# Odd layer of a 1024-token model: grouped heads before the latent ones, each set of heads prepared under other work

## The chip, the cores and the metric

One core of a Trainium2 chip runs the whole program in one launch. The metric is device microseconds of that core; less is better. Engines: TensorE (PE), VectorE (DVE), ScalarE (ACT), GpSimd (POOL); SyncE (SP) issues most of the transfers.

## The reference, cut to what matters

A first block (three mixers and a dense MLP) is followed by a second one of two layers, an even and an odd one, each a mixer and a mixture of 16 experts. The change is in the mixer of the odd layer, over 1024 tokens of width 1024:

```
def mixer_odd(h, pos, row, col, w_in, cq_norm, w_cq_up, ckv_norm, w_ckv_up, dq_norm, dk_norm, w_out):
    proj = h @ w_in                                   # 1184 columns
    cq, ckv, ck_rope, dq, dk, dv = jnp.split(proj, [o1, o2, o3, o4, o5], axis=-1)
    cq = (rmsnorm(cq, cq_norm) @ w_cq_up).reshape(b, s, C_HEADS, C_NOPE + C_ROPE)
    q_nope, q_rope = cq[..., :C_NOPE], rope(cq[..., C_NOPE:], pos, ROPE_THETA)
    kv = (rmsnorm(ckv, ckv_norm) @ w_ckv_up).reshape(b, s, C_HEADS, C_NOPE + C_V)
    k_nope, v_c = kv[..., :C_NOPE], kv[..., C_NOPE:]
    k_rope = rope(ck_rope, pos, ROPE_THETA)
    ...
    c_out = block_attention(q_c, k_c, v_c)
    dq = axial_rope(rmsnorm(dq.reshape(b, s, D_KV_HEADS, D_GROUP, HEAD_DIM), dq_norm), row, col)
    dk = axial_rope(rmsnorm(dk.reshape(b, s, D_KV_HEADS, HEAD_DIM), dk_norm), row, col)
    ...
    d_out = block_attention(dq, dk, dv)
    return jnp.concatenate([c_out, d_out], axis=-1) @ w_out
```

There are 8 latent heads (c: queries of 64 + 32 columns made from 256 low-rank columns, keys and values from 128) and 8 grouped heads (d: 64 columns, two heads of keys and values, four query heads to each). Softmax is over all 1024 keys.

## The kernel before

All matrices are float32; a product is made of three matmuls over operands split into a rounded high part and the rest (`mm3`, lines 91 to 93; `split_into`, lines 98 and 99: ACT copies the high part, DVE or POOL subtracts). Tokens lie on the partitions, in 8 tiles of 128.

Order of the odd layer in `program`: `norm_T` norms and transposes the rows into `h`; `odd_proj` makes the 1184 columns in five groups, the 416 latent ones into `cc` and then the 768 grouped ones into `dd`, and stops once between for `odd_c_in`, which norms the latent columns under the rest of the projections. `odd_c` transposes the low-rank columns (line 1744), and traces `odd_d_in` (norm and rotation of the grouped queries and keys, tile by tile, lines 1698 to 1702 and 1072 to 1077) at low priority. Then for each of two groups of four latent heads it makes the queries of all of them (line 1799), rotates them on POOL, and makes the values; each of these projections goes through the one PSUM bank `pj` and is read out of it by ACT and DVE. Head by head it stacks keys and queries (`stacks`) and runs the attention of the head before. Then the rows of the output weights are loaded and split (`w_rows`), and `odd_d` stacks the keys (line 369) and queries (line 361) of the grouped heads, a pair of heads at a time, and runs their attention. `out_moe` multiplies with the output weights, tile by tile; the 128 rows of the attention's output that come last (`late`) are loaded apart and used last.

`attn_head` takes a head in four units of two query tiles (256 rows). For each tile: scores into a pair of banks, the minimum (the queries are negated) on DVE (line 1038), exponential and sum on ACT (line 1041), transposition of the 1024 weights by PE (line 396) and their split (the second half by ACT and POOL, lines 400 to 402, into `pt`, of which there are three buffers). Then 16 matmuls with the values (lines 1048 and 1049), and the scaling, which POOL ends (line 1058) before the result goes to DRAM (`cD`, line 1060).

The order of the instructions on each engine is set before the run by a planner: it takes the order of the program text as priority and fills in, by estimated durations, what is ready by its own clock. On the chip each engine then works its list in that order.

Of the kernel before, what the change touches and what calls it, by code (L numbers as in the profile page):

```python
# [18 lines left out]
NT = 8  # L19
# [7 lines left out]
class Kern:  # L27
# [990 lines left out]
    def attn_head(self, sp, scores, V, dst, row, exp_scale, tab=None):  # L1018
# [3 lines left out]
        for qr in range(4):  # L1022
            pt = self.pt_tiles(sp, 3 if tab is None else 2)
            rc = sp.tile([128, 2], F32, name="arc", tag="arc", bufs=2)
            for qi in range(2):
# [5 lines left out]
                e = sp.tile([128, 1024], F32, name="e", tag="e", bufs=2 if tab is None else 3)  # L1031
                if tab is not None:
                    nc.vector.tensor_tensor_reduce(
                        out=e, in0=pv, in1=tab[:, 896 - 128 * t:1920 - 128 * t],
                        scale=1.0, scalar=3.0e38, op0=ALU.add, op1=ALU.min, accum_out=st[:, 0:1])
                    pv = e
                else:
                    nc.vector.tensor_reduce(out=st[:, 0:1], in_=pv, axis=AX.X, op=ALU.min)  # L1038
                    if exp_scale != 1.0:
                        nc.vector.tensor_scalar(st[:, 0:1], st[:, 0:1], exp_scale, None, op0=ALU.mult)  # L1040
# [648 lines left out]
    def rms_N(self, sp, x, n, g, sq=None):  # L1689

        nc = self.nc
        a = x.shape[1]
        if sq is None:
            sq = sp.tile([128, a * n], F32, name="rsq", tag="qn")
        sq = sq.rearrange("p (a n) -> p a n", a=a)
        ss = sp.tile([128, a], F32, name="rnss", tag="rnss%d" % a)
        rs = sp.tile([128, a], F32, name="rnrs", tag="rnrs%d" % a)
        nc.gpsimd.tensor_tensor(sq, x, x, op=ALU.mult)
        nc.vector.tensor_reduce(out=ss, in_=sq, axis=AX.X, op=ALU.add)
        self.rstd(ss, n, rs)  # L1700
        nc.vector.tensor_tensor(x, x, rs[:, :, None].to_broadcast([128, a, n]), op=ALU.mult)
# [12 lines left out]
    def rope_tab(self, sp, name, half, nh, free=None):  # L1714
        nc = self.nc
        r = []
        for i in range(2):
            if free is None:
# [470 lines left out]
```

## Time and profile before

| | |
|---|---|
| time, median of 3 runs | 4341.29 us (4339.98 to 4341.6) |
| the profiled execution | 4346.24 us, span 4344.5 us |
| PE busy | 3861.5 us, 89% |
| DVE, ACT, POOL busy | 2440.4, 1915.9, 1149.2 us |
| mean granted clock of PE | 0.939 of 2.4 GHz |

Busy time is what an engine spends in instructions; matmuls are pipelined, so a PE that is busy all the time can still be held up a little at each instruction. The span is from the first to the last instruction; the time of the execution is 1.7 us longer.

### The profile page before, as it was taken

What the parts mean: (1) busy time and instruction counts of PE and PEld (TensorE: products, weight loads), DVE (VectorE), ACT (ScalarE), POOL (GpSimd) and SP (SyncE); (2) the same over time, 40 slices, a digit from 0 to 9 for tenths busy, and PEclk for the clock granted to TensorE, in tenths of its full rate; (3) what the DMA queues carried; (4) which work ended last, traced back from release to release, by engine and by line L of the source; (5) the groups of instructions that cost most, each with busy time, mean ns of one, the idle gap of its engine ahead of it and who ended that gap; (6) DMA issues with size and microseconds to landing.
All of it is one profiled execution on the core that took longest, in us unless ns stands there. A gap on an engine that the chain in (4) does not pass through costs nothing. (4 is left out here: it accounts for less than half of the span.)

```text
span 4344.5 us, 57369 instructions
## 1 busy us (share of the span) xinstructions
PE 3861.5 (89%) x21765; PEld 3209.0 (74%) x21765; DVE 2440.4 (56%) x4070; ACT 1915.9 (44%) x3190; POOL 1149.2 (26%) x878
## 2 busy tenths in 40 slices
PE   6999978898799999998999988699895898996997
PEld 5887866666587888886899977576694787884765
DVE  6545584663344233336446673787538566736876
ACT  3444434241424211112455662366523667832765
POOL 2000041330343112124412221011024556620111
PEclk8999989989899999999899998799997999997999
DMA  4212253121543111112242333799410001036997
GB/s 167 72 51 56 85 177 102 49 99 54 203 146 97 54 44 54 44 49 80 61 120 74 85 88 128 280 377 361 150 45 9 18 8 58 19 103 248 375 356 245
DMA packets 321975, 531.40 MB, mean 122 GB/s; under 512 B 39894, under 2 KB 217441, under 8 KB 321700
## 3 DMA queue, kind: packets, MB, share of 16 engines
q1 hardware_dynamic: 312052, 492.62, 33.5%
q0 software_dynamic: 9648, 35.13, 3.2%
q8 instruction: 171, 2.80, 0.3%
q14 instruction: 104, 0.85, 0.1%
HBM read 427.39 MB, written 91.88 MB: 120 GB/s over the span
## 5 line engine op out<-in xcount | busy, mean ns | idle before, releaser
L98 ACT ACTIVATE whi<-wraw 128x1024 fp32r<-128x1024 f32 (+1 forms) x515 | 530.1, 1038 | 777.7 <-PE py L93 213.7
L99 DVE TENSOR_TENSOR wlo<-wraw,whi 128x1024 fp32r<-128x1024 f32 (+3 forms) x418 | 519.0, 1258 | 409.6 <-ACT whi L98 397.2
L99 POOL TENSOR_TENSOR wlo<-wraw,whi 128x1024 fp32r<-128x1024 f32 (+3 forms) x97 | 226.6, 2336 | 1198.0 <-ACT whi L98 1135.7
L91 PE MATMUL pj<-h,whi 128*128 128x512 f32 (+1 forms) x592 | 255.6, 432 | 44.0 <-ACT gst L791 41.8
L92 PE MATMUL mm<-h,whi 128*128 128x512 f32 x640 | 253.9, 397 | 3.0 <-POOL h L99 1.8
L91 PE MATMUL mm<-h,whi 128*128 128x512 f32 x640 | 252.7, 397 | 1.8 <-ACT ms L905 1.4
L93 PE MATMUL mm<-h,wlo 128*128 128x512 f32 x640 | 252.9, 396 | 0.8 <-POOL wlo L99 0.8
L92 PE MATMUL pj<-h,whi 128*128 128x512 f32 (+1 forms) x592 | 248.1, 419 | 0.0
L93 PE MATMUL pj<-h,wlo 128*128 128x512 f32 (+1 forms) x592 | 246.5, 416 | 0.2 <-POOL wlo L99 0.2
L91 PE MATMUL pgu<-whi,xe 128*128 128x512 f32 x512 | 207.6, 406 | 6.2 <-ACT xe L98 6.2
L927 DVE TENSOR_TENSOR Y<-py,Y 128x1024 f32<-128x1024 f32 x112 | 137.1, 1224 | 133.3 <-PE py L93 133.3
L91 PE MATMUL py<-whi,mr 128*128 128x512 f32 x512 | 201.6, 394 | 9.3 <-DVE mr L936 8.2
L93 PE MATMUL pgu<-whi,xe 128*128 128x512 f32 x512 | 205.7, 402 | 0.0
L92 PE MATMUL pgu<-wlo,xe 128*128 128x512 f32 x512 | 205.5, 401 | 0.0
L93 PE MATMUL py<-whi,mr 128*128 128x512 f32 x512 | 203.1, 397 | 0.0
L92 PE MATMUL py<-wlo,mr 128*128 128x512 f32 x512 | 202.4, 395 | 0.0
L396 PE MATMUL ptp<-ident,e 128*128 128x128 f32 x1280 | 183.8, 278 | 15.1 <-ACT pf L400 6.9
L1038 DVE TENSOR_REDUCE ast<-ps 128x1 f32<-128x1024 f32 x128 | 156.4, 1222 | 69.7 <-PE ps L93 48.6
L91 PEld LDWEIGHTS pj<-h,whi 128*128 128x128 f32 (+1 forms) x592 | 118.4, 200 | 85.4 <-ACT gst L791 50.7
L396 PEld LDWEIGHTS ptp<-ident,e 128*128 128x128 f32 x1280 | 149.9, 143 | 30.8 <-ACT pf L400 13.6
L402 POOL TENSOR_TENSOR pt<-pf,pt 128x512 fp32r<-128x512 f32 x128 | 164.0, 1281 | 10.4
L99 DVE TENSOR_TENSOR pt<-ptp,pt 128x512 fp32r<-128x512 f32 x192 | 130.5, 689 | 40.2 <-ACT pt L98 38.9
(643 smaller groups left out, 11038.2 us busy)
## 6 DMA issues: line engine op xcount, KB each, us to landing
wraw<-in_moe_w_gate_dram SPq DMA_DIRECT2D x128, 512.0 KB
wraw<-in_moe_w_up_dram SPq DMA_DIRECT2D x128, 512.0 KB
wraw<-in_moe_w_down_dram SPq DMA_DIRECT2D x128, 512.0 KB
wraw<-in_mlp_w_dram SPq DMA_DIRECT2D x64, 512.0 KB
wraw<-in_w_in_dram SPq DMA_DIRECT2D x52, 512.0 KB
wad<-in_ada_w_dram SPq DMA_DIRECT2D x48, 512.0 KB
gD<-gst SPq DMA_DIRECT2D x24, 512.0 KB
wraw<-x SPq DMA_DIRECT2D x20, 512.0 KB
```

The lines of the kernel that those rows point to most:

```text
L91: t.matmul(out, l[0], r[0], start=start, stop=False)
L92: t.matmul(out, l[0], r[1], start=False, stop=False)
L93: return t.matmul(out, l[1], r[0], start=False, stop=stop)
L98: nc.scalar.activation(hi, src, AF.Copy)
L99: (nc.gpsimd if leng == "pool" else nc.vector).tensor_tensor(lo, src, hi.bitcast(F32), op=ALU.subtract)
L396: nc.tensor.transpose(p[:, k, :], e[:, (4 * kg + k) * 128:(4 * kg + k + 1) * 128], self.ident)
L402: nc.gpsimd.tensor_tensor(lo, f, hi.bitcast(F32), op=ALU.subtract)
L927: nc.vector.tensor_tensor(y, pv, y, op=ALU.add)
L1038: nc.vector.tensor_reduce(out=st[:, 0:1], in_=pv, axis=AX.X, op=ALU.min)
```

## The change

The columns of the projection are reordered: keys and values of the grouped heads first, then their queries, and the latent columns last. The grouped keys and queries are normed and rotated under the following column groups, four tiles and up to four heads to an instruction instead of one tile and ten heads, and the keys are stacked there too. The grouped heads run first, the latent ones after them. `attn_head` calls a function at the beginning of each of its units; `program` and `odd_c` hold tables of what is made at which unit: the norms of the latent columns in units 1 to 3 of the grouped heads, their transposes in 5 to 7, the first group's queries, rotation and values in 9 to 15, the shared key part in 17, and the first latent head's stacks in 25 and 26. In the latent heads, each head's stacks come some units ahead, the second group's queries in units 9 to 11 and its values in 12 and 13. The rows of the output weights are loaded one at a time in seven latent units, and the eighth after the attention. Tiles are in other places of the memory; the last rows of the attention's output are now the fourth 128 (`late` is 3, was 7). The even layer calls the new `w_rows` for the same eight rows.

```
-    def attn_head(self, sp, scores, V, dst, row, exp_scale, tab=None):
+    def attn_head(self, sp, scores, V, dst, row, exp_scale, step, unit):
...
+            step(unit + qr)
+            pt = self.pt_tiles(sp, 3)
...
+        a, b = x.shape[1:3]
+        g = g[:, None, None, :].to_broadcast([128, a, b, n])
...
+            sq = sp.tile([128, 1024], F32, name="rsq", tag="rsq")
+        sq = sq[:, :a * b * n].rearrange("p (a b n) -> p a b n", a=a, b=b)
+        ss = sp.tile([128, a * b], F32, name="rnss", tag="rnss%d" % (a * b))
+        rs = sp.tile([128, a * b], F32, name="rnrs", tag="rnrs%d" % (a * b))
...
+        nc.vector.tensor_reduce(out=ss.rearrange("p (a b) -> p a b", a=a), in_=sq, axis=AX.X, op=ALU.add)
...
+        rs = rs.rearrange("p (a b) -> p a b", a=a)[:, :, :, None].to_broadcast([128, a, b, n])
+        nc.vector.tensor_tensor(x, x, rs, op=ALU.mult)
...
-        for i, (c0, lo) in enumerate(((0, 0), (160, 256), (416, 416), (672, 672), (928, 928))):
-            if i == 2:
-                yield
+        for i, (c0, lo) in enumerate(((928, 928), (416, 416), (672, 672), (0, 0), (160, 256))):
...
+            if lo >= 416:
+                yield
...
-    def odd_c_in(self, cc, sp):
...
-        with self.low_priority():
-            meanwhile()
...
+        g = [self.row(a[nm], 64, nm, sp) for nm in ("odd_dq_norm_2", "odd_dk_norm_2")]
+        return g, [self.rope_tab(sp, nm, 16, 4) for nm in ("rope_row", "rope_col")]
...
+    def odd_d_in(self, dd, h0, nh, g, tabs, sp):
+
+        for t in range(0, NT, 4):
+            x = dd[:, t:t + 4, h0 * 64:(h0 + nh) * 64].rearrange("p t (h c) -> p t h c", h=nh)
+            self.rms_N(sp, x, 64, g)
             for j in range(2):
...
+                self.rope_N(sp, x[:, :, :, o:o + 16], x[:, :, :, o + 16:o + 32],
+                            *[y[:, t:t + 4, 0:nh] for y in tabs[j]])
...
+    def odd_d(self, dd, V, KK, Q, dst, skq, sp, step):
+        for h in range(8):
+            kv, q = h // 4, Q[h % 2]
+            if h % 2 == 0 and h < 6:
+                nxt = self.odd_queries(skq)
+                self.pair_stacks(lambda t: dd[:, t, (h + 2) * 64:(h + 4) * 64], "q", nxt, -0.125)
             self.attn_head(sp, lambda p, t: self.scores(p, q, KK[kv][0], KK[kv][1], t),
...
+                           lambda k: V[:, k, kv, :], dst, 512 + h * 64, 1.0, step, 4 * h)
+            if h % 2:
+                Q = nxt
...
+    def odd_c_in(self, cc, tabs, sp):
...
+        f = sp.tile([128, NT * 384], F32, name="cin", tag="qn")
+        g = []
+        for nm, o, n in (("odd_cq_norm_2", 1024, 256), ("odd_ckv_norm_2", 1280, 128)):
+            g.append(f[:, o:o + n])
+            nc.sync.dma_start(g[-1], dap(a[nm], 0, [[0, 128], [1, n]]))
+
+        def norm(i, t):
+            o, n = ((0, 256), (256, 128))[i]
+            self.rms_N(sp, cc[:, t:t + 4, o:o + n].rearrange("p t (h c) -> p t h c", h=1), n, g[i], f)
...
+    def odd_c(self, cc, tabs, dst, skq, sc, sq, sp, done):
...
+        def ranks(j, gq):
+            p = self.pj()
+            for t in range(4):
+                nc.tensor.transpose(p[:, t * 128:(t + 1) * 128], cc[:, 4 * gq + t, j * 128:(j + 1) * 128], self.ident)
+            self.split_into(p, *[(cv[i][:, 0] if j == 2 else cq[i][:, j])[:, gq * 512:(gq + 1) * 512] for i in range(2)])
...
+        def queries(hg, t):
+            if t == 0:
+                w = self.whalf(*[self.wsrc(a["odd_w_cq_up_2"], 128 * k, 1, 384 * hg, 384) for k in range(2)])
+                wq[hg] = self.parts(w, 384, n=2)
+                qn[hg] = sc.tile([128, NT, 384], F32, name="qn", tag="qn")
+            p = self.pj()
+            self.proj_N(wq[hg], cq, t, p[:, 0:384])
+            nc.scalar.activation(qn[hg][:, t, :], p[:, 0:384], AF.Copy)
...
+        def values(hg, t2):
...
+            p = self.pj()
+            for u in range(2):
+                self.proj_N(wv[hg], cv, 2 * t2 + u, p[:, u * 256:(u + 1) * 256])
+            pv = p.rearrange("p (u h c) -> p u h c", u=2, h=4)
+            for i in range(2):
+                self.split_into(pv[:, :, 2 * i:2 * i + 2], *[V[hg][i][:, 2 * t2:2 * t2 + 2, :, o:o + 64] for o in (0, 64)])
...
+        def stacks(h):
+            return [lambda f=f, g=g: f(h, g) for g in range(2) for f in (stack_q, stack_k)]
+        steps = lambda f, *xs: [lambda x=x: f(*x) for x in xs]
+        group = lambda hg: (steps(queries, *[(hg, t) for t in range(NT)]), steps(rotate, (hg, 0), (hg, 4)),
+                            steps(values, *[(hg, t) for t in range(4)]))
+        (q0, r0, v0), (q1, r1, v1) = group(0), group(1)
+        ready = [steps(ranks, *[(j, g) for j in (2, 0, 1) for g in range(2)]),
+                 q0[:4] + r0[:1] + q0[4:] + r0[1:] + v0, steps(key_tile, (0,)), stacks(0)]
+        order = {0: steps(key_tile, (1,)) + stacks(1), 4: stacks(2)[:2], 5: stacks(2)[2:], 8: stacks(3)[:2], 9: stacks(3)[2:] + q1[:2],
+                 10: q1[2:4] + r1[:1] + q1[4:6], 11: q1[6:] + r1[1:] + [done], 12: v1[:2], 13: v1[2:] + stacks(4)[:2],
+                 14: stacks(4)[2:]}
+        for h in (5, 6, 7):
+            order[4 * h - 4], order[4 * h - 3] = stacks(h)[:2], stacks(h)[2:]
...
+        def run(step):
+            def both(u):
+                for f in order.get(u, ()):
+                    f()
+                step(u)
...
+                self.attn_head(sp, qk, lambda k: V[h // 4][h % 4 // 2][:, k, h % 2, :], dst, h * 64, 96.0 ** -0.5, both, 4 * h)
+        return ready, run
...
+        dd = opn("dd").tile([128, NT, 768], F32, name="dd")
+        V = opn("dv").tile([128, NT, 2, 128], FR, name="dvv")
         cc = opn("cc").tile([128, NT, 416], F32, name="cc")
+        skq = opn("kq", "right")
...
+        (gq, gk), tabs = self.odd_d_consts(sd)
+        proj = self.odd_proj(h, a["odd_w_in_2"], cc, dd, (self.wp, 2, 2, opn("pw")))
+
         next(proj)
-        self.odd_c_in(cc, sd)
+        self.odd_d_values(dd, V)
+        self.odd_d_in(dd, 8, 2, gk, tabs, sd)
+        next(proj)
+        self.odd_d_in(dd, 0, 4, gq, tabs, sd)
+        next(proj)
+        KK = self.odd_keys(skq)
+        self.pair_stacks(lambda t: dd[:, t, 512:640], "k", KK)
+        self.odd_d_in(dd, 4, 4, gq, tabs, sd)
         for _ in proj:
             pass
+        Q = self.odd_queries(skq)
+        self.pair_stacks(lambda t: dd[:, t, 0:128], "q", Q, -0.125)
...
-        self.odd_c(cc, cD, opn("oy"), sp, lambda: self.odd_d_in(dd, V, sp, cc.rearrange("p t c -> p (t c)")))
-        cls("oy", "cc")
-        hl = opn("ow")
-        wl = self.w_rows("odd_w_out_2", hl)
-        self.odd_d(dd, V, cD, sp)
-        cls("oc", "dv", "dd")
+        sc, sq = opn("oy", "right"), opn("oq", "right")
...
+            cls("oq")
+            OW.append(opn("ow1"))
+
+        def rows_of_out(k):
+            self.w_rows("odd_w_out_2", OW[-1], wl, k)
+        tabs = self.rope_tab(sc, "rope_odd", 16, 4)
+        inp = self.odd_c_in(cc, tabs, sc)
+        (ranks, first, key, head), run = self.odd_c(cc, tabs, cD, skq, sc, sq, sp, low_ranks_used)
+        order = {1: inp[:2], 2: inp[2:3], 3: inp[3:]}
+        for i, f in enumerate(ranks):
+            order.setdefault(5 + i // 2, []).append(f)
+        for i, f in enumerate(first):
+            order.setdefault(9 + i // 2, []).append(f)
+        for u, f in ((17, key), (25, head[:2]), (26, head[2:])):
+            order.setdefault(u, []).extend(f)
...
+        self.odd_d(dd, V, KK, Q, cD, skq, sp, step)
+        cls("cc", "dv", "dd")
+        OW.append(opn("ow"))
+        order = {4: [0], 6: [1], 8: [2], 15: [3], 18: [4], 20: [5], 22: [6]}
+        run(lambda u: [rows_of_out(k) for k in order.get(u, ())])
+        cls("oy", "oc", "kq")
+        OW.append(opn("ow2"))
+        rows_of_out(7)
...
+        self.out_moe(1, wl, ("ow2", "ow1", "ow"), cD, 3, x3, x5, h6, opn, cls, banks, finish, "right")
...
+    def w_rows(self, name, hl, wl, k):
+
+        hi, lo = [hl.tile([128, 1024], FR, name="%s%d" % (n, k)) for n in ("wrh", "wrl")]
+        raw = self.wp.tile([128, 1024], F32, name="wraw", tag="wraw", bufs=2)
+        self.nc.sync.dma_start(raw, self.a[name][128 * k:128 * k + 128, :])
+        self.split_into(raw, hi, lo, leng=self.lo_engine())
+        wl.append(self.parts((hi, lo), 512))
```

## Rows read from the trace of the kernel before

**Rows 1.** the head of the page and its first part: busy time of each engine, its share of the span, and instructions.

```profile
span 4344.5 us, 57369 instructions
...
PE 3861.5 (89%) x21765; PEld 3209.0 (74%) x21765; DVE 2440.4 (56%) x4070; ACT 1915.9 (44%) x3190; POOL 1149.2 (26%) x878
```

**Rows 2.** busy us of each engine (and instructions) by stretch. Columns: the stretch, its length, PE, PE's weight loads, DVE, ACT, POOL, PE's granted clock (1.00 is 2.4 GHz), the mean busy share of the DMA engines, GB/s.

```profile
3123.00:3245.00 122.00, 121.38 (x1025) 120.49 (x1026) 47.48 (x82) 37.79 (x76) 25.04 (x13) 0.98 0.20 53
3245.00:3330.00 85.00, 35.71 (x145) 24.51 (x143) 71.77 (x167) 23.17 (x57) 37.85 (x26) 0.65 0.09 18
3330.00:3430.00 100.00, 98.42 (x636) 88.76 (x636) 64.19 (x130) 71.01 (x140) 57.59 (x62) 0.98 0.07 18
3430.00:3501.00 71.00, 53.74 (x309) 44.16 (x309) 34.36 (x66) 36.58 (x74) 28.80 (x32) 0.88 0.03 6
...
3600.00:3661.00 61.00, 48.04 (x288) 40.21 (x288) 43.68 (x63) 46.18 (x84) 36.84 (x35) 0.89 0.31 94
3661.00:3761.00 100.00, 95.85 (x670) 85.36 (x669) 72.59 (x117) 82.81 (x164) 70.17 (x79) 0.98 0.05 12
```

**Rows 3.** POOL's timeline, the lines of L1058: the multiply that ends an attention unit, 64 in all, latent heads first. Columns: start us, us, engine, line, operation, tiles and shapes, count; in brackets the idle time before it and what ended it.

```profile
3389.75 0.74 POOL L1058 TENSOR_TENSOR fo<-fo 64x256 f32<-64x256 f32 x1 [1.23 <-DVE fo L1057]
...
3447.26 0.74 POOL L1058 TENSOR_TENSOR fo<-fo 64x256 f32<-64x256 f32 x1 [1.17 <-DVE fo L1057]
...
3465.11 0.73 POOL L1058 TENSOR_TENSOR fo<-fo 64x256 f32<-64x256 f32 x1 [2.96 <-DVE fo L1057]
...
3501.09 0.74 POOL L1058 TENSOR_TENSOR fo<-fo 64x256 f32<-64x256 f32 x1 [1.17 <-DVE fo L1057]
...
3581.30 0.74 POOL L1058 TENSOR_TENSOR fo<-fo 64x256 f32<-64x256 f32 x1 [1.22 <-DVE fo L1057]
...
3587.97 0.73 POOL L1058 TENSOR_TENSOR fo<-fo 64x256 f32<-64x256 f32 x1 [1.22 <-DVE fo L1057]
...
3609.56 0.72 POOL L1058 TENSOR_TENSOR fo<-fo 64x256 f32<-64x256 f32 x1 [1.61 <-DVE fo L1057]
...
3632.19 0.72 POOL L1058 TENSOR_TENSOR fo<-fo 64x256 f32<-64x256 f32 x1
...
3690.37 0.73 POOL L1058 TENSOR_TENSOR fo<-fo 64x256 f32<-64x256 f32 x1 [0.75 <-DVE fo L1057]
...
3696.24 0.73 POOL L1058 TENSOR_TENSOR fo<-fo 64x256 f32<-64x256 f32 x1 [0.75 <-DVE fo L1057]
...
3703.06 0.72 POOL L1058 TENSOR_TENSOR fo<-fo 64x256 f32<-64x256 f32 x1 [4.13 <-DVE fo L1057]
...
3712.73 0.73 POOL L1058 TENSOR_TENSOR fo<-fo 64x256 f32<-64x256 f32 x1 [0.70 <-DVE fo L1057]
...
3829.50 0.73 POOL L1058 TENSOR_TENSOR fo<-fo 64x256 f32<-64x256 f32 x1 [4.65 <-DVE fo L1057]
```

**Rows 4.** PE's timeline after the projections, columns as before: the first transposes of the latent columns, two matmuls of the values' projection after waits, the first scores.

```profile
3244.92 1.04 PE L1744 MATMUL tp<-ident,cc 128*128 128x128 f32 x8
...
3275.58 0.58 PE L92 MATMUL pj<-wlo,cT 128*128 128x256 f32 x1 [8.78 <-POOL wlo L99]
...
3291.35 0.55 PE L91 MATMUL pj<-whi,cT 128*128 128x256 f32 x1 [14.34 <-DVE rnrs L170]
...
3314.87 1.22 PE L91 MATMUL ps<-ck,cq 96*128 96x512 f32 x2 [0.68 <-ACT ck L98]
```

**Rows 5.** the timelines of POOL (one line) and DVE (two lines) in the same stretch: the gain multiply of the grouped norm, and two products of the rotation.

```profile
3269.91 1.53 POOL L1702 TENSOR_TENSOR dd<-dd,cc 128x640 f32<-128x640 f32 x1 [9.29 <-issue]
...
3271.47 1.36 DVE L1072 TENSOR_TENSOR cc<-dd,cc 128x160 f32<-128x160 f32 x1 [7.94 <-POOL dd L1702]
...
3282.95 0.31 DVE L1072 TENSOR_TENSOR cc<-dd,cc 128x160 f32<-128x160 f32 x1
```

**Rows 6.** instructions that touch the tiles cc (latent columns) and qn (latent queries). Columns: line, engine, operation, tiles, count: shortest/median/longest ns, first and last start us; shapes.

```profile
L1698 POOL TENSOR_TENSOR rsq<-cc x4: 1040/1496/2502, 3151.4 to 3180.1; 128x1024 f32<-128x1024 f32 x2, 128x512 f32<-128x512 f32 x2
...
L1702 POOL TENSOR_TENSOR cc<-cc,odd_cq_norm x2: 2387/2392/2396, 3160.9 to 3168.4; 128x1024 f32<-128x1024 f32 x2
...
L1722 SPq DMA_DIRECT2D cc<-in_rope_col_dram x2: 469/1572/2675, 3248.3 to 3250.5; - x2
...
L1799 ACT ACTIVATE qn<-pj x16: 472/491/498, 3250.8 to 3423.7; 128x384 f32<-128x384 f32 x16
L1072 POOL TENSOR_TENSOR rp<-qn,rope_odd x2: 1357/1382/1407, 3275.5 to 3424.2; 128x512 f32<-128x512 f32 x2
```

**Rows 7.** timelines again: PE, the first and sixth matmul of one query projection, two value steps of the second group, the first grouped scores; DVE, one subtraction of an output weight.

```profile
3264.46 0.45 PE L91 MATMUL pj<-whi,cT 128*128 128x384 f32 x1 [1.03 <-ACT qn L1799]
...
3265.46 0.34 PE L93 MATMUL pj<-whi,cT 128*128 128x384 f32 x1
...
3465.41 0.38 PE L91 MATMUL pj<-whi,cT 128*128 128x256 f32 x1 [1.89 <-DVE cv L99]
...
3468.29 0.55 PE L91 MATMUL pj<-whi,cT 128*128 128x256 f32 x1 [1.90 <-DVE cv L99]
...
3610.25 0.80 PE L379 MATMUL ps<-K,Q 128*128 128x512 f32 x1 [4.30 <-DVE Q L362]
...
3606.51 2.52 DVE L99 TENSOR_TENSOR wlo<-wraw,whi 128x1024 fp32r<-128x1024 f32 x1 [1.33 <-ACT whi L98]
```

**Rows 8.** the page's costliest groups: the first half of a weight's split, over the whole program. Columns: line, engine, operation, tiles and shapes, count | busy us, mean ns of one | idle before, releaser.

```profile
L98 ACT ACTIVATE whi<-wraw 128x1024 fp32r<-128x1024 f32 (+1 forms) x515 | 530.1, 1038 | 777.7 <-PE py L93 213.7
```

More of the change, by code (lines that the diff above doesn't have):

```diff
@@ L1030, in attn_head @@
                 pv = p.rearrange("p a b -> p (a b)")
[L1031 to L1040, printed above, removed]
+                e = sp.tile([128, 1024], F32, name="e", tag="e", bufs=2)
+                nc.vector.tensor_reduce(out=st[:, 0:1], in_=pv, axis=AX.X, op=ALU.min)
+                if exp_scale != 1.0:
+                    nc.vector.tensor_scalar(st[:, 0:1], st[:, 0:1], exp_scale, None, op0=ALU.mult)
                 nc.scalar.activation(e, pv, AF.Exp, bias=st[:, 0:1], scale=-exp_scale, accum_out=st[:, 1:2])
@@ L1723, in rope_tab, with odd_d_consts @@
             r.append(t[:, :, None, :].to_broadcast([128, NT, nh, half]))
         return r
[L1726 removed]
+    def odd_d_consts(self, sp):
         a = self.a
[L1729 to L1734 removed]
@@ new lines, in odd_queries @@
+    def odd_queries(self, sp):
+        return [sp.tile([128, 1024], FR, name="Q%d" % i, tag="Q", bufs=4) for i in range(2)]
+    def odd_d(self, dd, V, KK, Q, dst, skq, sp, step):
[4 more added lines that the diff above has]
+                self.pair_stacks(lambda t: dd[:, t, (h + 2) * 64:(h + 4) * 64], "q", nxt, -0.125)
+            self.attn_head(sp, lambda p, t: self.scores(p, q, KK[kv][0], KK[kv][1], t),
+                           lambda k: V[:, k, kv, :], dst, 512 + h * 64, 1.0, step, 4 * h)
+            if h % 2:
+                Q = nxt
@@ new lines, in odd_c_in, with key @@
+    def odd_c_in(self, cc, tabs, sp):
+        nc, a = self.nc, self.a
+        f = sp.tile([128, NT * 384], F32, name="cin", tag="qn")
[6 more added lines that the diff above has]
+            self.rms_N(sp, cc[:, t:t + 4, o:o + n].rearrange("p t (h c) -> p t h c", h=1), n, g[i], f)
+        def key():
+            kr = cc[:, :, 384:416].rearrange("p t (h c) -> p t h c", h=1)
+            self.rope_N(sp, kr[:, :, :, 0:16], kr[:, :, :, 16:32], *[x[:, :, 0:1] for x in tabs], free=f[:, 1408:1792])
+        return [lambda: norm(1, 0), lambda: norm(1, 4), lambda: norm(0, 0), lambda: norm(0, 4), key]
@@ L1996, in last @@
             hl = opn("eT", "right")
-            T.extend((self.w_rows("even_w_out_2", hl), "eT"))
+            T.extend(([], ("eT",)))
+            for k in range(8):
+                self.w_rows("even_w_out_2", hl, T[0], k)
         self.even_attn(h, a["even_w_in_2"], eD, s1, W2, between, last)
@@ new lines, in program, with step @@
+        (ranks, first, key, head), run = self.odd_c(cc, tabs, cD, skq, sc, sq, sp, low_ranks_used)
[6 more added lines that the diff above has]
+            order.setdefault(u, []).extend(f)
+        def step(u):
+            for f in order.get(u, ()):
+                f()
@@ L2100, in out_moe @@
             banks(False)
-        cls(hl)
+        cls(*hl)
         mw = opn("mw", "left" if side == "right" else "right")
```

191 lines of the change are left out of this document (57 added, 134 removed).

## Prediction

> **What bounds it now.** I read the page first: TensorE (PE) is busy 89% of 4344.5 us [rows 1], so most of the program can't shrink by moving work of other engines. Then the stretches around the odd attention [rows 2]: the projections (3123 to 3245) keep PE busy 121 of 122 us at clock 0.98, but the next 85 us hold 35.7 us of PE work at clock 0.65, while VectorE (DVE) is busy 71.8. Two more stretches are thin: 3430 to 3501 (53.7 of 71) and 3600 to 3661 (48.0 of 61). Third, PE's own timeline inside the first hole [rows 4]: it waits 8.8 us for a split on POOL and 14.3 us for DVE, and the first scores start at 3314.9, 70 us after the projections. Fourth, what DVE did there: the norm and rotation of the grouped heads, which the attention then running (the latent heads) doesn't need; DVE itself first waits 7.9 us for POOL, whose gain multiply waited 9.3 us [rows 5]. Last, the ends of the 64 attention units [rows 3], a unit being two query tiles of one head, ended by POOL's multiply on L1058. Undisturbed they follow each other every 6.67 us (latent, 3581.30 to 3587.97) and 5.87 us (grouped, 3690.37 to 3696.24). In the grouped stretch PE is busy 95.9 of 100 us and ScalarE (ACT) 82.8 [rows 2]: PE sets the unit, ACT stands next.
>
> **What 128 steady units would not need.** The 63rd unit ends at 3829.50 [rows 3], 584.5 us after the projections. 32 units at 5.87 and 31 at 6.67 are 395 us. The other 190 us are PE work of the preparation and waiting. I count the same 63 units anew.
>
> **The change, part by part.** *Columns reordered, grouped heads normed under the later columns.* The same five column groups, so the same PE time, and they still start when the first normed rows come: the projections end at 3245 again. They leave DVE 122 − 47.5 = 74.5 us free; everything that DVE did in the hole was 71.8 [rows 2], and the moved part is less than that, now in fewer, wider instructions. The keys are normed three groups before they are used, the last queries one group. Cost 0; without that cover up to 72 us, which is the old hole. Their tables and gains are moved ahead of the weights of later columns on SP: the slowest table issue took 2.7 us [rows 6], six loads, while PE works on weights that are there; 0. The copies that complete the key stacks go the same way; the latent tables and gains are issued as the grouped units start and are needed a unit later.
>
> *Start of the grouped attention.* What is late after the projections is now one query stack and a pipeline fill. Before, the grouped start took 22.6 us from one unit's end to the next (3609.56 to 3632.19), with a 4.3 us PE wait for the query stack [rows 3, 7], among six weight splits: ACT 1.04 us each [rows 8] and DVE up to 2.5 [rows 7], which are gone from there. Bounds: two unit lengths, 12, and 22.6 + 4.3 = 27. Nearer the upper, whose conditions are alike but for the splits: 20 to the first unit's end.
>
> *Grouped units:* 31 further at 5.87 = 182.
>
> *Their later query stacks:* around one of them two units took 9.67 + 6.82 us [rows 3], 4.7 over two plain ones. PE's part is 8 transposes, 1.04 us [rows 4]. Three of them: 3 to 14, I take 12.
>
> *Latent preparation between grouped units.* PE: 32 transposes at 1.04 per eight = 4.2; eight query projections of six matmuls, 1.0 us from first to sixth start [rows 7], some 1.05 each = 8.4; four value steps, some 0.75 each = 3; one head's stacks, eight transposes and six matmuls of 512 columns (a latent unit has four more of these than a grouped one and is 0.80 longer, so 0.2 each) = 2.2. Sum 18, no longer in a hole but in PE's own time. Waiting comes on top, as all these steps share one PSUM bank, which must be read out before its next use. The nearest row: the six units over which the second group's queries and one stack are made, 3389.75 to 3447.26, took 57.5 instead of 40.0 [rows 3], 17.5 for 10.6 of PE work, a factor 1.65. So 30. Behind PE's wait stand the scores of the next unit, and behind them DVE's minimum and ACT's exponential. The norms of the latent columns: four squares (median 1.5 us, up to 2.5) and four gain multiplies (2.39 the wide, half that the narrow) on POOL [rows 6], 14 us; over three units POOL has 3 × 5.87 × 0.3 = 5 us free (70.2 of 100 busy [rows 2]), the third buffer of transposed weights covers one unit, and some 4 us remain. The rotation, twelve ops of half of 1.4 us [rows 6], fits. ACT gains eight copies of 0.49 [rows 6] and some 20 like them, about 14 us in the 34 that the stretch grows: no busier than its 0.83, below PE. Together 34; bounds 18 (no waiting) and 34 + 29, for which see the value steps below.
>
> DVE's rotation op took 1.36 us when a POOL op lay beside it and 0.31 without [rows 5]; the weights' subtraction 2.52 [rows 7]. The Trainium skill (SBUF — State Buffer, "Who interferes with whom") says that a VectorE instruction with two SBUF inputs contends with a GpSimd one that reads SBUF, the later blocking fully, while one with a PSUM input does not. By that rule POOL's 14 us of norms cost DVE's reductions in the units nothing, and only the subtractions of the output weights pay; by the rows alone each of some 25 DVE ops beside them could pay 1 us, 25 us more. The rows can't tell the two inputs apart; I keep the 4.
>
> *Latent units:* 31 at 6.67 = 206.8. No start of its own: keys and queries of its first head are ready during grouped head 6. Seven stacks, 2.2 of PE work each: 15, with waits 21. *Second group* (queries, values): 11.4 × 1.65 = 19, spread over heads 2 and 3. Before, its values stood alone between two heads: 3465.11 to 3501.09, 36.0 instead of 6.67, where PE waits 1.9 us for each bank [rows 3, 7]. That is the 29 us which I take as gone, since other units now stand between; it is the upper bound if they don't.
>
> *Output weights between latent units, the eighth after them.* Seven splits: ACT 1.04 [rows 8] with a quarter of its time free; the subtraction, if DVE's next reduction stands behind it, up to 2.5 [rows 7]: 0 to 16 in all, I take 5, as a unit leaves DVE a third of its time. The eighth, some 3.5 us after the attention, stands beside the first output products of six other rows; 0 to 3. Two shorter loads instead of one for each output tile: 0, PE is at work there. The even layer's weights: same loads, same splits, 0.
>
> **The sum.** 20 + 182 + 12 + 34 + 206.8 + 21 + 19 + 5 = 500 against 584.5: 85 us less. The profiled execution took 4346.2, the median is 5 below it: 4341.3 − 85 = 4257. All lower bounds: 12 + 182 + 3 + 18 + 206.8 + 15 + 11.4 = 448, 136 less, 4205. All upper: 27 + 182 + 14 + 63 + 206.8 + 21 + 48 + 19 = 581, 4 less, 4338. What follows (output products, expert layer) starts from the same point relative to the attention's end, since its buffers come free there in both.
>
> **The rivals.** *The preparation hides better than the row of the second group says* (17%). For it: steady units leave DVE and POOL 30% free, and the steps are now two or three a unit. Against: one bank. Half of the waits and of the start's excess gone: 4220 to 4235, down to 4205.
>
> *The value steps still stand alone* in one group or in both (17%). For it: their order on PE comes from a planner's estimate, and their bank wait of 1.9 us was there before. 29 or 58 us back: 4286 to 4315.
>
> *The change doesn't do what it says* (5%): the grouped norms on DVE and POOL still end after the projections, or the preparation is planned ahead of the first units; then all upper bounds come together, 4338, within 0.2%.
>
> *Slower* (5%): PE's clock. In the stretches where PE waits, the granted clock is 0.65, 0.88 and 0.89, in the other three 0.98 [rows 2]; after the 8.8 and 14.3 us waits the matmuls run at the 1.2 GHz level (0.58 us against 0.38 for the same shape [rows 4, 7]). For it: waits of only 1.9 us, one after another, did the same (0.55 at 3468.29). If the steps break the grouped stretch so often that it runs at the hole's 0.65, its 182 + 34 us become 216 × 0.98 / 0.65 = 326: 110 more, 4367. It decides from an average of 0.70 (85 us). Against: with the second group's queries between units the stretch 3330 to 3430 kept 0.98. The Trainium skill (TensorE: Matmul & The Clock Gate, "HAM oscillation") describes kernels whose engine falls back at every wait for data; the two holes agree, 3330 to 3430 does not.
>
> **How the numbers follow.** The sum has 56%, with 4235 to 4282 as its own range. Leaving out the slower case, the unchanged one and the ends of the two others gives 4215 to 4308 for 8 in 10. Faster by over 0.2% (9 us, what a measurement of this kernel can tell): 56 + 17 + 17 = 90%; the same 5%, slower 5%.
>
> **What would show it.** Right: after the projections PE idles less than 10 us at a stretch, clock above 0.9 throughout; the first 32 unit ends belong to the grouped rows of the output, every 5.9 us many of them 1 to 3 us longer, followed without a gap by latent ones; DVE and POOL busier in the projections by some 30 and 10 us. Wrong: a unit interval over 20 us in the value steps (second rival); the norms of the grouped queries after the last projection (third); PEclk under 0.8 in the grouped stretch (fourth); or a gain lost behind the attention, if the first output tile waits for the eighth row of weights.

## The result and the profile after

The changed kernel took 4268.4 us, median of 4 runs (4265.6 to 4278.4), the kernel before beside it 4340.7: a ratio of 0.984 (95% interval 0.982 to 0.9855), 72 us less. Measured once more (e10), the two took 4263.6 and 4347.0, a ratio of 0.982 (0.980 to 0.984). The forecast was 4257, its range 4215 to 4308.

The stretches of the changed kernel, by windows of its trace: projections, start, further grouped units, latent units (columns: window, length, busy time of PE, PEld, DVE, ACT and POOL with their instructions, granted clock, DMA share, GB/s). They answer [rows 2] of the kernel before.

```profile
3123.00:3257.00 134.00, 127.95 (x1028) 126.99 (x1029) 86.30 (x169) 41.73 (x86) 35.26 (x18) 0.94 0.23 64
3257.00:3291.00 34.00, 26.47 (x122) 20.89 (x120) 31.50 (x57) 20.87 (x45) 20.60 (x16) 0.70 0.16 41
3291.00:3502.00 211.00, 202.70 (x1429) 182.35 (x1429) 156.59 (x253) 173.53 (x347) 151.87 (x168) 0.99 0.08 19
3502.00:3759.00 257.00, 241.50 (x1593) 213.32 (x1594) 162.80 (x313) 182.69 (x362) 157.65 (x174) 1.00 0.09 23
```

DVE and POOL are 39 and 10 us busier in the projections than before, and the 85 us hole at clock 0.65 has shrunk to 34 us at 0.70. From there PE is busy for 95% of the time, and no wait of it that the trace shows is longer than 3.2 us.

The POOL operation that ends a unit, in the timeline of the changed kernel (it answers [rows 3]; as there, a unit's end is counted at the start of this operation): units 1, 16, 17, 32, 33, 43, 44, 48, 49 and 63.

```profile
3290.93 0.73 POOL L1053 TENSOR_TENSOR fo<-fo 64x256 f32<-64x256 f32 x1
...
3397.01 0.72 POOL L1053 TENSOR_TENSOR fo<-fo 64x256 f32<-64x256 f32 x1 [2.94 <-DVE fo L1052]
3410.77 0.72 POOL L1053 TENSOR_TENSOR fo<-fo 64x256 f32<-64x256 f32 x1 [0.77 <-DVE fo L1052]
...
3501.72 0.72 POOL L1053 TENSOR_TENSOR fo<-fo 64x256 f32<-64x256 f32 x1 [4.34 <-DVE fo L1052]
3510.67 0.74 POOL L1053 TENSOR_TENSOR fo<-fo 64x256 f32<-64x256 f32 x1 [1.15 <-DVE fo L1052]
...
3593.78 0.73 POOL L1053 TENSOR_TENSOR fo<-fo 64x256 f32<-64x256 f32 x1 [2.27 <-DVE fo L1052]
3606.76 0.73 POOL L1053 TENSOR_TENSOR fo<-fo 64x256 f32<-64x256 f32 x1
...
3636.96 0.72 POOL L1053 TENSOR_TENSOR fo<-fo 64x256 f32<-64x256 f32 x1 [5.49 <-DVE ast L1035]
3651.80 0.72 POOL L1053 TENSOR_TENSOR fo<-fo 64x256 f32<-64x256 f32 x1
...
3759.32 0.73 POOL L1053 TENSOR_TENSOR fo<-fo 64x256 f32<-64x256 f32 x1
```

The longest interval is 14.84 us (unit 49, where the second group's values lie), where it was 36.0. The 63rd unit ends at 3759.32 instead of 3829.50. The layer starts at another time in each profiled execution (its first transposes on L259 at 3115 to 3128 us, ahead of all that the change touches), so the table counts from there, from the rows of each trace.

| us after the layer's start | last projection matmul | unit 1 | unit 32 | unit 63 | from unit 63 to the end | median of the runs |
|---|---|---|---|---|---|---|
| before | 121.8 | 222.1 | 486.5 | 706.5 | 515.0 | 4340.7 |
| changed | 132.8 | 166.3 | 377.1 | 634.7 | 509.3 | 4268.4 |
| changed, again (e10) | 132.2 | 165.2 | 375.9 | 633.4 | 509.6 | 4263.6 |
| e1 norms held | 124.1 | 224.1 | 436.0 | 695.0 | 519.3 | 4335.4 |
| e2 preparation last | 130.5 | 154.7 | 360.3 | 689.4 | 519.2 | 4331.4 |
| e3 two half tiles | 132.2 | 165.4 | 376.2 | 631.0 | 508.9 | 4265.3 |
| e5 one value tile | 132.8 | 166.2 | 377.2 | 631.8 | 513.0 | 4267.8 |
| e9 values before keys | 132.1 | 165.4 | 375.9 | 650.5 | 511.7 | 4286.4 |
| e4 keys early | 127.5 | 160.9 | 369.8 | 627.2 | 512.1 | 4272.2 |
| e6 rows spaced | 132.5 | 165.7 | 373.4 | 630.4 | 515.6 | 4268.7 |
| e7 norms held, keys early | 127.6 | 150.6 | 375.9 | 636.2 | 512.3 | 4274.0 |
| e8 all three | 127.2 | 148.8 | 367.1 | 626.6 | 514.3 | 4264.4 |
| e11 keys and rows | 127.5 | 160.8 | 367.4 | 625.4 | 518.3 | 4264.0 |

The whole gain, 71.8 us, is there at unit 63. (In the kernel before, unit 32 is the last latent one.) The column behind it runs from 508.9 to 519.3 us, so that 8 us at unit 63 can't be seen in the whole time of single executions. It isn't scatter alone: behind unit 63, DVE and ACT work through their instructions in the same order in the changed kernel, e10, e2, e4 and e7 (509.3 to 519.2 us), but in another one in e1, e6, e8 and e11 (514.3 to 519.3 us). The planner makes its order anew for each edited program, so an edit can change it far behind its own place.

### The profile page after: what moved, and what is told of

The parts are those of the page before. It is cut to its first block, busy times and chain, and to the rows that moved or that the text cites. A ratio compares the mean times of both kernels' runs of the same rounds, so it can differ in the third digit from the quotient of the medians.

```text
span 4268.6 us, 57274 instructions
## 1 busy us (share of the span) xinstructions
PE 3842.8 (90%) x21765; PEld 3204.3 (75%) x21765; DVE 2430.1 (57%) x4033; ACT 1909.5 (45%) x3185; POOL 1150.4 (27%) x886
## 5 line engine op out<-in xcount | busy, mean ns | idle before, releaser
L98 ACT ACTIVATE whi<-wraw 128x1024 fp32r<-128x1024 f32 (+2 forms) x497 | 512.7, 1040 | 761.5 <-PE py L93 213.7
L99 DVE TENSOR_TENSOR wlo<-wraw,whi 128x1024 fp32r<-128x1024 f32 (+2 forms) x409 | 501.7, 1243 | 375.6 <-ACT whi L98 363.6
L99 POOL TENSOR_TENSOR wlo<-wraw,whi 128x1024 fp32r<-128x1024 f32 (+2 forms) x88 | 207.3, 2356 | 1152.3 <-ACT whi L98 1089.4
L1033 DVE TENSOR_REDUCE ast<-ps 128x1 f32<-128x1024 f32 x128 | 156.3, 1221 | 43.7 <-PE ps L93 30.7
L396 PEld LDWEIGHTS ptp<-ident,e 128*128 128x128 f32 x1280 | 150.5, 142 | 32.5 <-ACT pf L400 14.8
L99 DVE TENSOR_TENSOR pt<-ptp,pt 128x512 fp32r<-128x512 f32 x192 | 130.0, 686 | 46.4 <-ACT pt L98 45.3
```

Source lines behind the costliest of these rows:

```text
L98: nc.scalar.activation(hi, src, AF.Copy)
L99: (nc.gpsimd if leng == "pool" else nc.vector).tensor_tensor(lo, src, hi.bitcast(F32), op=ALU.subtract)
L396: nc.tensor.transpose(p[:, k, :], e[:, (4 * kg + k) * 128:(4 * kg + k + 1) * 128], self.ident)
```

## The experiments

Several of them hold a step back with a gate: a one-column copy on POOL from a tile that is written at the wanted moment into the tile that the step writes first. The step then depends on that moment, and the planner can't put it earlier.

**e1: the grouped norms behind the projections.**

```
+        hold = sd.tile([128, 1024], F32, name="rsq", tag="rsq")
+        nc.gpsimd.tensor_copy(hold[:, 0:1], cc[:, 7, 415:416])
```

> The changed kernel, but the norms of the grouped columns may start only when the last projected column group has been read out (a one-column POOL copy from the low-rank columns into the scratch of the squares makes them wait); heads, steps and everything else as changed. Theory (the gain at the start is the cover that the later columns give): VectorE's and GpSimd's share of some 39 and 10 us leaves the projections, of which the keys and the first four heads stand ahead of the first scores; the first grouped unit ends 55 to 80 us after the projections instead of 33.5, the projections themselves end some 8 us earlier, and the whole takes 4285 to 4320 us. Rival (the gain comes from the wider and fewer instructions, wherever they lie): first unit within 10 us of 33.5, the whole 4258 to 4278.

Measured: 4335.4 us, ratio 0.998 (0.997 to 0.999): nearly all of the gain is gone. The projections end 8.7 us sooner, as expected, but unit 1 ends 100 us after them, later than the 55 to 80 expected; the latent norms stand among the grouped ones on DVE there. The stretch between, by windows of this run:

```profile
3248.00:3348.00 100.00, 29.85 (x117) 22.30 (x117) 95.04 (x170) 23.95 (x57) 43.82 (x29) 0.56 0.10 25
```

DVE is busy 95 of 100 us and PE 30, at clock 0.56. From unit 1 to 32 it takes 211.9 us, the changed kernel 210.8: nothing of this is given back. The wider instructions alone were not the gain, their cover was.

**e2: the latent preparation behind the grouped units.**

```
+        def hold():
+            for o in (0, 1408):
+                nc.gpsimd.tensor_copy(f[:, o:o + 1], self.rc[:, 0:1])
...
+        for f in inp + ranks + first + key + head:
+            f()
```

`self.rc` is a small tile that each attention unit writes anew; `hold` stands first in `inp`.

> The changed kernel, but the whole preparation of the latent heads (their norms, transposes, queries, values, first stacks) may start only when the last grouped units run (its scratch is first written from a tile of one of these). Theory (the preparation is cheap only between units): between the last grouped and the first latent unit a hole of 45 to 70 us opens, the grouped stretch shrinks from 211 us to 190 to 197, and the whole takes 4295 to 4325 us. Rival (the preparation costs the grouped units as much as it would cost alone, so that its place doesn't matter): hole under 30 us, the whole 4260 to 4280.

Measured: 4331.4 us, ratio 0.997 (0.996 to 0.9985). The unit ends 30 to 33, in the timeline of POOL in this run:

```profile
3466.37 0.75 POOL L1053 TENSOR_TENSOR fo<-fo 64x256 f32<-64x256 f32 x1
3478.87 0.73 POOL L1053 TENSOR_TENSOR fo<-fo 64x256 f32<-64x256 f32 x1
3488.10 0.72 POOL L1053 TENSOR_TENSOR fo<-fo 64x256 f32<-64x256 f32 x1
3568.84 0.74 POOL L1053 TENSOR_TENSOR fo<-fo 64x256 f32<-64x256 f32 x1 [1.17 <-DVE fo L1052]
```

The last interval is 80.7 us, longer than the 45 to 70 expected. From unit 30 to unit 33 it takes 102.5 us instead of 20.6 in the changed kernel, so the preparation in one piece costs 82. In the changed kernel it costs 15.2 in units 1 to 30 (199.1 against 183.9) and 9.3 at the start (33.5 against 24.2 from the last projection matmul to unit 1), together 24.5. Between the units it costs 57 us less than alone.

The two gates give back 60.3 (e1) and 54.7 us (e2) at unit 63, together far more than the 71.8 gained. The old hole of 85 us held both at once, latent preparation on PE and grouped norms on DVE [rows 4, 5]; with only one of them hidden, and the rest of the change in place, 11.5 and 17.1 us of the gain are left.

**e3, e5, e9: where the former 36 us interval came from.** e3 takes one of the three half-group value tiles away (bufs=2), e5 has one whole tile as before, and e9 also writes the next head's stacks behind the values. In all three v1[:1] only loads the weights.

```
-                V[hg] = [sc.tile([128, NT, 2, 128], FR, name="cv", tag="cv", bufs=3) for _ in range(2)]
+                V[hg] = sc.tile([128, NT, 4, 128], FR, name="cv", tag="cv")
```

Order of the steps in e5 (its end), then in e9:

```
+                 10: q1[2:4] + r1[:1] + q1[4:6], 11: q1[6:] + r1[1:] + [done], 12: v1[:1], 13: stacks(4)[:2],
+                 14: stacks(4)[2:], 16: v1[1:]}
...
+                 10: q1[2:4] + r1[:1] + q1[4:6], 11: q1[6:] + r1[1:] + [done], 12: v1[:1], 16: v1[1:] + stacks(4)}
```

> The changed kernel with two instead of three half-group value tiles, so that the second group's last value tile can be written only when latent head 3 is done, as the one value tile of the kernel before forced it for all of them; the value steps are moved to that place. Theory (the former hole of 36 us, 29 more than a unit, came from the buffer): one unit interval there of 25 us or more, the whole 4283 to 4300 us. Rival (it came from the steps standing in a row on PE, which they don't here): no interval over 18 us, the whole 4262 to 4276.

> The changed kernel with one value tile for all four heads of a group, as the kernel before had it, and the second group's value steps written at latent head 4; the rest as changed. Theory (the former 36 us interval came from the whole tile: every value step had to wait for head 3's last weighted sum and head 4's first one for every value step, so that nothing could stand between; half tiles take that away, be they two or three): an interval of 25 us or more at latent head 4's first unit, the attention 15 to 30 us longer, the whole 4282 to 4300 us. Rival (the planner slips units between the value steps with one tile too): no interval over 20 us, the whole 4262 to 4278.

> As the run with one value tile, but the first stacks of latent head 4 are written behind the second group's value steps, as in the kernel before. Theory (the former hole is an order of PSUM banks and queues: the value steps wait for the one tile, the key stack of the next head stands behind them on the same bank and in PE's queue, and the next scores behind the key stack): an interval of 30 us or more at the first unit of latent head 4, the attention 18 to 30 us longer than in the changed kernel, the whole 4286 to 4300 us. Rival (steps in a row don't cost more than steps between units): no interval over 20 us, the whole 4262 to 4274.

Measured: e3 4265.3 (0.982, 0.980 to 0.984) and e5 4267.8 (0.9825, 0.981 to 0.984), no slower than the changed kernel; their longest intervals are 17.8 and 17.5 us. My first two theories fell: the number of buffers didn't make the hole. e9 took 4286.4 (0.987, 0.985 to 0.989); it differs from e5 only in the order of steps, and is 18.6 us longer, 18.7 at unit 63. Units 48 and 49 in the timeline of POOL in e9:

```profile
3629.61 0.72 POOL L1053 TENSOR_TENSOR fo<-fo 64x256 f32<-64x256 f32 x1 [3.40 <-DVE fo L1052]
3666.89 0.72 POOL L1053 TENSOR_TENSOR fo<-fo 64x256 f32<-64x256 f32 x1
```

and PE's timeline between them:

```profile
3629.91 0.39 PE L91 MATMUL pj<-whi,cvT 128*128 128x256 f32 x1 [2.10 <-DVE cv L99]
...
3632.88 0.55 PE L91 MATMUL pj<-whi,cvT 128*128 128x256 f32 x1 [1.90 <-DVE cv L99]
...
3636.40 0.55 PE L91 MATMUL pj<-whi,cvT 128*128 128x256 f32 x1 [1.90 <-DVE cv L99]
...
3639.92 0.66 PE L91 MATMUL pj<-cvT,whi 128*64 128x512 f32 x1 [1.90 <-DVE cv L99]
...
3642.11 1.22 PE L91 MATMUL ps<-ck,Q 96*128 96x512 f32 x2 [0.68 <-ACT ck L98]
```

The interval is 37.3 us, and the rows are those of [rows 7] again: value step, wait of 1.9 us for the one bank, value step, then the key stack on the same bank, and only then the first scores. The scores start 12.5 us after unit 48 has ended, and unit 49 ends another 24.8 us later, about what unit 1 takes behind the projections in e2 (24.2): the pipeline of units has run empty and fills anew, which costs more than the bank waits themselves. With the stacks written ahead of the values the scores of head 4 go on between the value steps, with one tile too, as PE's timeline in e5 shows:

```profile
3635.40 0.29 PE L91 MATMUL pj<-whi,cvT 128*128 128x256 f32 x1
...
3637.26 0.48 PE L91 MATMUL ps<-ck,Q 96*128 96x512 f32 x1
...
3639.57 0.37 PE L91 MATMUL pj<-whi,cvT 128*128 128x256 f32 x1
...
3641.68 0.50 PE L91 MATMUL ps<-ck,Q 96*128 96x512 f32 x1 [0.28 <-ACT e L1036]
```

Against the changed kernel the net loss at unit 63 is 16 us, a little under the 18 to 30 expected: units 46 to 48 are shorter (14.1 us together instead of 20.2), as the value steps are gone from them.

**e4: the key stacks one column group earlier.**

```
         next(proj)
+        KK = self.odd_keys(skq)
+        self.pair_stacks(lambda t: dd[:, t, 512:640], "k", KK)
         self.odd_d_in(dd, 0, 4, gq, tabs, sd)
         next(proj)
-        KK = self.odd_keys(skq)
-        self.pair_stacks(lambda t: dd[:, t, 512:640], "k", KK)
```

> The changed kernel with the key stacks made one column group earlier, ahead of the norm of the first four query heads in program order. Theory (PE's 4.4 us wait at 3220 is a chain of queues: the key stack's subtraction stands on VectorE behind rotations that wait for GpSimd, ScalarE's copy for it, and the read-out of projected columns behind that on ScalarE): the wait and the half-clock matmuls after it are gone, the projections end 5 to 9 us sooner, the whole takes 4259 to 4264 us. Rival (VectorE and GpSimd slow each other wherever the stack lies): another wait of the same length appears, projections' end and the whole within 3 us of the changed kernel, 4265 to 4272.

The chain in the changed kernel's timeline (all engines, rows left out):

```profile
3207.66 2.40 POOL L1699 TENSOR_TENSOR dd<-dd,odd_dq_norm 128x1024 f32<-128x1024 f32 x1 [7.32 <-DVE dd L1698]
3207.97 1.06 ACT L369 ACTIVATE K<-tp 64x512 fp32r<-64x512 f32 x2
...
3210.02 2.40 POOL L99 TENSOR_TENSOR wlo<-wraw,whi 128x1024 fp32r<-128x1024 f32 x1
3210.10 2.60 DVE L1067 TENSOR_TENSOR rp<-dd,rope_row 128x256 f32<-128x256 f32 x1 [2.52 <-POOL dd L1699]
3212.38 2.08 POOL L1694 TENSOR_TENSOR rsq<-dd 128x1024 f32<-128x1024 f32 x1
3212.63 2.11 DVE L1068 TENSOR_TENSOR rp<-dd,rope_row 128x256 f32<-128x256 f32 x1
3214.66 0.41 DVE L1069 TENSOR_TENSOR rp<-dd,rope_row 128x256 f32<-128x256 f32 x1
...
3217.47 0.68 DVE L370 TENSOR_TENSOR K<-tp,K 64x512 fp32r<-64x512 f32 x1
...
3218.18 0.59 ACT L369 ACTIVATE K<-tp 64x512 fp32r<-64x512 f32 x1 [9.15 <-DVE K L370]
...
3219.73 0.60 ACT L1706 ACTIVATE cc<-mb 128x512 f32<-128x512 f32 x1
...
3220.38 0.58 PE L91 MATMUL mb<-whi,ho 128*128 128x256 f32 x1 [4.41 <-ACT cc L1706]
```

DVE's key subtraction (L370) stands behind the rotations, ACT's next key copy waits 9.15 us for it, and the read-out of projected columns behind that copy keeps PE from its bank for 4.41 us. Behind the wait the granted clock was 0.51 for 6.3 us, the 1.2 GHz level, by a window of the same trace:

```profile
3220.30:3226.60 6.30, 6.22 (x29) 6.22 (x30) 4.66 (x10) 0.94 (x4) 0.81 (x1) 0.51 0.54 118
```

In e4 PE's longest wait for a read-out in the projections is 1.1 us; they end 5.3 us sooner, unit 63 ends 7.5 us sooner. The mechanism is as I thought; the whole time doesn't show it: 4272.2 us, ratio 0.983 (0.9815 to 0.985), above the 4259 to 4264 expected. The profiled execution was the shortest of its five, 4262.2; the others took 4270.5 to 4273.0.

**e6: rows of output weights spaced.** The new argument `after` gives a tile of the unit before.

```
         hi, lo = [hl.tile([128, 1024], FR, name="%s%d" % (n, k)) for n in ("wrh", "wrl")]
+        if after is not None:
+            self.nc.gpsimd.tensor_copy(hi[:, 0:1], after[:, 0:1])
```

> The changed kernel, but each row of output weights is split only when the latent unit has come at which it is written (a one-column POOL copy from a tile of the unit before into its destination); in the changed kernel three rows lie together in grouped unit 17 and three in latent unit 44. Theory (bunched splits cost more than the 5 us that I gave all rows): units 16 and 17 take 16 to 18 us together instead of 23.3, unit 44 under 10 instead of 13.0, the 63rd unit ends 8 to 14 us sooner after the layer's start, the whole 4254 to 4262 us. Rival (a split costs a unit the same wherever it lies, a few us in sum): the 63rd unit within 4 us of the changed kernel's, the whole 4264 to 4272.

Three splits within units 16 and 17 of the changed kernel, with their subtractions on POOL and DVE, and the wait of PE's transposes behind them (timeline, all engines):

```profile
3390.58 2.00 ACT L98 ACTIVATE wrh<-wraw 128x1024 fp32r<-128x1024 f32 x2
3391.71 2.37 POOL L99 TENSOR_TENSOR wrl<-wraw,wrh 128x1024 fp32r<-128x1024 f32 x1 [1.51 <-ACT wrh L98]
...
3392.64 2.51 DVE L99 TENSOR_TENSOR wrl<-wraw,wrh 128x1024 fp32r<-128x1024 f32 x1
...
3396.02 1.24 PE L396 MATMUL ptp<-ident,e 128*128 128x128 f32 x8 [3.19 <-DVE Q L362]
...
3398.88 1.05 ACT L98 ACTIVATE wrh<-wraw 128x1024 fp32r<-128x1024 f32 x1
```

Measured: units 16 and 17 take 15.7 instead of 23.3 us and unit 44 takes 8.7 instead of 13.0, as the theory said; but units 18 to 32 take 95.4 instead of 91.0 and unit 49 takes 19.9 instead of 14.8. Unit 63 ends 4.3 us sooner instead of 8 to 14, the whole is the same, 4268.7 (0.983, 0.981 to 0.984). The rival is nearer: most of it comes back elsewhere.

**e7, e8, e11: combinations.** e7 has the gate of e2 at unit 4, with the steps behind it written three units later, and the keys of e4; e8 adds e6; e11 is e4 with e6, run beside e10, the changed kernel again.

> The changed kernel with the key stacks one column group earlier (as in the run on the keys alone) and the latent norms held until grouped unit 4 (their scratch is first written from a tile of unit 3). Theory (VectorE is full at the start of the attention, and what is not needed there is worth its whole time): the first grouped unit ends 12 to 17 us sooner after the layer's start than in the changed kernel (167.1 us), the norms cost units 4 to 8 at most 5 us, the 63rd unit ends 9 to 14 us sooner, the whole 4253 to 4260 us. Rival (the norms cost as much between the units): first unit 12 to 17 sooner, but the 63rd only by the 5 to 7 us of the keys, the whole 4260 to 4268.

> The changed kernel with key stacks early, latent norms held until unit 4 and rows of output weights spaced: a candidate to beat the changed kernel. Theory: the gains of the two runs before it add up, 63rd unit 17 to 28 us sooner after the layer's start than the changed kernel's 635 us, the whole 4241 to 4253 us. Rival (they take the same idle time, so that only the larger counts): 63rd unit 9 to 14 us sooner, the whole 4253 to 4262.

> The changed kernel itself, beside the next one on the same chip: 4264 to 4272 us, and in its profile the 63rd unit again 633 to 637 us after the layer's start, with the same intervals.

> The changed kernel with the key stacks one column group earlier and the rows of output weights spaced, the latent norms left as they are. Theory (keys 5 and rows 4 us are separate waits and add up, and holding the norms gave back what it brought): the 63rd unit 8 to 13 us sooner after the layer's start than in the changed kernel, the whole 5 to 12 us below the changed kernel of the same call. Rival (the holding was part of the gain of all three): 63rd unit less than 6 us sooner, the whole within 5 us.

Measured: e7 took 4274.0 us (0.983, 0.982 to 0.9845). Unit 1 ends 15.7 us sooner than in the changed kernel, but units 2 to 17 take 9.5 us more, 18 to 32 another 5.0 and the latent ones 2.7, and unit 63 ends 1.5 later: worse than the rival had it. What the norms leave at the start, they take between the units. The pairs that differ in the norms alone say so: from e4 to e7 the start shortens by 10.4 us and units 2 to 17 lengthen by 11.2; from e11 to e8 it is 11.7 and 11.1.

e8 took 4264.4 (0.981, 0.980 to 0.982) and e11 4264.0 (0.981, 0.979 to 0.983) with unit 63 8 to 9 us sooner than in the changed kernel, against 4263.6 for e10, which was run beside e11. For e8 that is less than its theory (17 to 28) and its rival (9 to 14) had. At unit 63 keys and rows add up; in the whole none beats the changed kernel measurably. In e11's profiled execution the part behind unit 63 took 8.7 us more than in e10's, and 7.8 of them lie behind the last matmul of the experts. There ACT waits for rows that POOL gathers (timelines of ACT, e10 and then e11):

```profile
4238.95 1.06 ACT L174 ACTIVATE wraw<-wraw 128x1024 f32<-128x1024 f32 x1 [5.00 <-DMA wraw<-x,idx]
...
4248.99 1.06 ACT L174 ACTIVATE wraw<-wraw 128x1024 f32<-128x1024 f32 x1 [13.57 <-DMA wraw<-x,idx]
```

e11 is one of the kernels with the other order of instructions behind unit 63, so the edit itself may have cost there what it won before. That isn't shown: e2 and e4, which keep the changed kernel's order, took 23.6 and 23.9 us behind the last expert matmul, e11 25.2 and e10 17.4. Order or scatter stays open.

No run puts the rows of output weights back into one block between the two kinds of heads, or leaves the latent heads first; what these two parts of the change brought by themselves isn't shown.

## Why the forecast came out

Counted from 3245 the sum put unit 63 at 3745; it ended at 3759.3. The mechanism was right, work of DVE and of the one bank hidden under PE's own, but that the sum came so near is in part luck: its terms were off by up to 17 us, and in both directions.

- **Projections, 0 in the sum: 12.6 us** (3244.8 to 3257.4). 1.6 is the later start of the layer in this execution, 11.0 remain. The step "Cost 0" looked at DVE's free time, which was enough, and not at what the key stacks stand behind in the queues of DVE and ACT. The wait of 4.4 us and the time lost at the lower clock behind it (half of the 6.3 us, some 3, an estimate) are most of this. e4 gives 5.3 back, e1, without norms and stacks there, 8.7; the last 2.3 us stay unexplained.
- **Start, 20: 33.5.** I had put the latent norms into the units. The planner puts them where an engine looks free to it, and that was the start, where DVE is busy 31.5 of 34 us. Held back, the start took 24.2 (e2) and 23.0 (e7), DVE was busy 17.3 us of it in either, and the granted clock was 0.86 and 0.85 instead of 0.70.
- **Grouped units, their stacks and the preparation, 182 + 12 + 34 = 228: 210.8.** The factor 1.65 on 18 us of PE work was the mistake: e2 shows 15.2 us for it, about its PE work alone. With the start's 9.3 the preparation cost 24.5, so the first rival (it hides better) was half right. That the start and the grouped units together come out at 244.3 against 248 is two errors that nearly cancel.
- **Latent units, 206.8 + 21 + 19 + 5 = 252: 257.6.** About right in sum. Its seven stacks were given a factor of 1.4 for waits, not the 1.65 of the steps beside them, without a reason. And the 5 us for rows of weights stood for seven separate splits; four are split together in units 44 and 45, and three, earlier than written, in grouped units 16 and 17.
- **The values, 29 us taken as gone:** they are, and e9 brings the interval of 37.3 back. My reason was short: units go on between the value steps only because the keys are written first (e5 against e9).
- **Behind the attention, 0:** 5.7 us less than in the execution before, within the spread of that column.

Of the rivals, the values alone and the unchanged one are refuted by intervals of at most 14.84 us and by grouped norms whose last rotations lie at 3228 to 3232, before the projections end; the slower one by the clock, which was 0.99 and 1.00 in the units. Only the start ran at 0.70, which "above 0.9 throughout" got wrong.

The rows before couldn't tell whether POOL's norms slow DVE's reductions. The changed kernel's can: its minima, which read PSUM, in the view of line L1033 (shortest, median and longest in ns):

```profile
L1033 DVE TENSOR_REDUCE ast<-ps x128: 1204/1225/1226, 3264.1 to 3748.5; 128x1 f32<-128x1024 f32 x128
```

None is longer, though some lie beside POOL's gain multiplies, as the last pair of these rows does (timelines of DVE and POOL):

```profile
3277.13 2.34 POOL L1694 TENSOR_TENSOR cin<-cc 128x1024 f32<-128x1024 f32 x1
3277.72 1.78 DVE L165 TENSOR_SCALAR rsv<-rnss 128x4 f32<-128x4 f32 x1
...
3282.52 1.21 DVE L1695 TENSOR_REDUCE rnss<-cin 128x4 f32<-128x1024 f32 x1
3282.61 1.28 POOL L1699 TENSOR_TENSOR cc<-cc,cin 128x512 f32<-128x512 f32 x1 [1.32 <-DVE rsv L169]
...
3286.21 1.21 DVE L1033 TENSOR_REDUCE ast<-ps 128x1 f32<-128x1024 f32 x1
3286.73 2.39 POOL L1699 TENSOR_TENSOR cc<-cc,cin 128x1024 f32<-128x1024 f32 x1
```

The rotation in the chain above, with both inputs in SBUF, took 2.60 and 2.11 us beside a POOL operation and 0.41 (L1069) without. Both agree with the rule of the Trainium skill (SBUF — State Buffer, "Who interferes with whom") that the prediction gives. The middle pair shows that a reduction out of SBUF isn't longer either, and the first that another kind of operation on one SBUF tensor is, so reading PSUM need not be what spared the minima. The 25 us more that the rows alone allowed didn't come.

## What to carry to other kernels

Work that is hidden under a full TensorE can be worth most of its length: the grouped norms lengthen the start by 66.5 us when they stand alone (e1) and were worth 60 at unit 63, and the latent preparation takes 82 us alone (e2) and 24.5 between units, even though it brings TensorE work of its own. When two such pieces filled one hole, both have to go. But "the engine is free" is not enough: what each moved instruction stands behind on its queue and PSUM bank has to be followed to the next matmul. Where steps share one bank, write what the next unit needs first ahead of what it needs later, so that the pipeline doesn't run empty. A few us won in the middle should be counted at a marker behind the change and from one ahead of it, and even then they may not reach the end, where the order of instructions can have changed with the edit.

## What was not expected of the hardware

The DVE rotation of 128x256 took 2.60 us instead of 0.41 beside a POOL operation of 2.40 (L99, from 3210.02): it ended 0.3 us after that did. The ACT copy that waited 9.15 us stood behind the key subtraction, which came eight instructions after this rotation on DVE. Small operations aren't spared: the one at 3277.72 above, on four columns and with one tensor as input, took 1.78 us instead of 0.16 and ended when POOL's did.

The intervals between unit ends mostly repeat to 0.1 us between executions of the same instruction order (13.0 for unit 44 in nine of the thirteen profiled kernels, those that leave the rows as changed); between the changed kernel and e10 the largest differences are 0.8 us, in units 3 and 17. The stretches with the expert layers spread over 10 us.
